# Two mixer sections reordered: input tiles and gates moved ahead of the RWKV scores and of the first chain

## The chip, the cores and the metric

The kernel runs on one core of a Trainium2 chip. The metric is the device time of one execution in microseconds (us), the median of several runs. The core has five engines with a queue of instructions each: PE (TensorE, matrix products), DVE (VectorE), ACT (ScalarE), POOL (GpSimd) and SP (SyncE, which here issues nearly all DMAs). Each works through its own queue in order, and they wait for one another through semaphores.

## The reference, cut to what matters

A hybrid encoder of two layers on 256 positions of 1024 channels, in fp32. Each layer is FFN, token mixers, FFN; the mixers are three branches on one shared input, weighted by gates:

```python
def hybrid_mixer(h, ...):                       # h: (1, 256, 1024)
    proj = h @ w_in                             # all branches' inputs and the gates
    ya = rwkv7_mixer(proj[..., :o1], ...) @ pa_w
    yb = hyena_mixer(proj[..., o1:o2], ...) @ pb_w
    yc = ssd_mixer(proj[..., o2:o3], ...) @ pc_w
    gates = jax.nn.sigmoid(proj[..., o3:]).reshape(bsz, L, N_BRANCH, D_MODEL)
    merged = gates[:, :, 0] * ya + gates[:, :, 1] * yb + gates[:, :, 2] * yc
    return merged @ w_out

def rwkv7_step(S, inp):                         # 256 steps, two directions, 8 heads of 64
    r_t, w_t, k_t, v_t, a_t, b_t = inp
    sa = jnp.einsum('dbhij,dbhj->dbhi', S, a_t)
    S = S * w_t[..., None, :] + sa[..., None] * b_t[..., None, :] + v_t[..., None] * k_t[..., None, :]
    return S, jnp.einsum('dbhij,dbhj->dbhi', S, r_t)
```

The sublayers are modulated by vectors that are themselves products of a condition with `ada_w` (`mod = cond @ ada_w[l] + ada_b[l]`). They don't depend on `x`, so the kernel computes those of later sublayers as side work.

## The kernel before, in words

`mixers(l)` writes one layer's mixers in program order; a scheduler in the framework then decides, from that order and its own estimates, in which order each engine gets its instructions. What follows is the order that came out.

The RWKV recurrence is done in chunks of 64 positions, for four heads at a time: wave 0 and wave 1. A wave has five steps. `rw_proj` computes its six input tiles; `rw_keys` the decays and keys (DVE, ACT, POOL); `rw_scores` the chunks' score matrices on PE, written to DRAM as `zin`; `rw_invert` loads `zin`, inverts triangular 32x32 blocks in 30 steps on POOL (lines 919 and 921) and stores `zout`; `rw_chain` loads `zout`, forms the chunks' inverses with 32x32 products and then goes through four chunks, one after the other. `rw_out` normalises and scales the result (a mean and a variance by matmul, DVE and ACT steps between).

Beside this stands dense work. Every column tile of `w_in` is one unit: 512 KB of weights are loaded on SP into one of four buffers named `raw` (`plain`), then PE does eight 128x256 fp32 matmuls into one of four banks (`psd`). A layer's mixers have 9 units for the RWKV inputs, 24 gates, 1 + 12 for the SSD branch (`ssd_proj`, `ssd_tiles`) and 12 for the Hyena branch (`hy_proj`). A gate is a unit, a tanh on ACT (`go`) and a store to DRAM (`gate`); `merge` loads it back as `gi`. In `merge`, the branch outputs, split into two fp32r halves (`yx`), are multiplied with the branch's output matrix (`whi`, `wlo`, loaded from `in_pab`), 8 units for each of the three branches.

`SEQ` says in which order the dense units stand behind the RWKV part in the program: ten gates, `ssd_proj` and the SSD tiles, then, after `ssd`, fourteen gates and the eight Hyena steps. Between the latter the side work (`side_work`) is spread, with a ring of three 512 KB buffers that lie where the SSD inputs were (`blk`).

The order of a mixer section on PE before the change, by the scheduler's result: inputs of wave 0, scores 0, inputs of wave 1, gates, scores 1 among gates, the rest of ten gates and the first SSD units, chain 0, chain 1 with the other dense units among their steps, output of wave 1 among the last Hyena units and the first merges, hyena, the other merges, `wout`.

Small tiles come from pools: `pt` from one that lives through the sublayer, `lt` from one that is opened after `self.arena.drop()`, in space that the arena of the RWKV part has given back.

Of the kernel before, what the change touches and what calls it, by code (L numbers as in the profile page):

```python
# [13 lines left out]
F32R = mybir.dt.float32r  # L14
# [10 lines left out]
K0 = math.exp(-0.5)  # L25


ARENA, AHEAD, BLK, START = 63 * 256, 65 * 256, 7 * 1024, 16 * 1024

KEEP, GRID = ("blk", "y0", "y1", "mg"), 256  # L30

# [8 lines left out]

NSIDE, NRING, SPOOL, NRAW, SIDEM = (4, 2, 4, 4, 1, 1), 3, (0, 0, 0, 0, 1, 0, 1, 0), 4, 3

SEQ = ("g" * 10 + "d" + "s" * 12, "g" * 14 + "h" * 8)

REL = (0, 0, 0, 0, 0, 0)

# [165 lines left out]
class Builder:  # L212
# [52 lines left out]
    def A(self, name, *shape):  # L265
        return self.arena.take(name, shape)

    def F(self, *names):
        self.arena.give(names)
# [812 lines left out]
        self.ya.append(y)  # L1082

    def out_split(self, y):
        yx = self.pt("yx", [2, 2, 256], 2, F32R)
        self.split(yx[:, 0], yx[:, 1], y)
        return [(yx[:, 0, p, :], yx[:, 1, p, :]) for p in (0, 1)]

# [55 lines left out]
    def ssd(self, l):  # L1144
        nc, A, F, bank, scol = self.nc, self.A, self.F, self.bank, self.scol

        self.yc = []
        for g in (0, 1):
            xd = A("xd", 2, 2, 256)
# [23 lines left out]
            for p in (0, 1):  # L1173
                h = 4 * g + 2 * p
# [19 lines left out]
                            self.mm(py[64 * e:64 * e + 64, p, ts], xd[:, c, d, hs], ws[:, e, n, :], n == 0, n == 2)  # L1194
                    F(f"sws{t}")
                F("svb")
            y = A("sy", 2, 256)
            for p in (0, 1):
                j = 2 * g + p
                self.stt(y[:, p, :], self.sx[:, j, :], self.dh[:, j:j + 1], py[:, p, :], MUL, ADD)  # L1200
# [7 lines left out]
            self.rsqrt(rs)  # L1208
            for p in (0, 1):
                self.stt(y[:, p, :], y[:, p, :], self.pc(l, "snw", 2 * g + p), rs, MUL, MUL)  # L1210
            self.yc += self.out_split(y)
            F("scb", "sy", "ssq", "srs", "xd")


    def hy_sin(self, x):
# [155 lines left out]
    def mixers(self, l):  # L1371
        A = self.A
        with self.phase("q") as pool:
            self.arena_open((self.pp, ARENA), (pool, AHEAD))
            blk = self.arena.sub("blk", BLK)
            st = [None, None]
            self.gd, self.mh = [None] * 3, []
            self.relief = REL[0]
            self.proj_pair(l)
            self.zz, self.ztmp = A("zz", 32, 32), A("ztmp", 240)[0:64]  # L1380
            self.rw_begin(l)
            st[0] = self.rw_proj(l, 0)
            self.rw_keys(st[0])
            self.rw_scores(st[0])
            st[1] = self.rw_proj(l, 1)
            self.relief = REL[1]
            self.rw_invert(st[0])
            self.rw_keys(st[1])
            self.rw_scores(st[1])
            self.rw_invert(st[1])  # L1390
            self.rw_chain(st[0])
            self.rw_out(st[0])
            self.F("zz", "ztmp")
            self.rw_chain(st[1])
            self.rw_out(st[1])
        self.arena.drop()
        with self.phase("w") as self.wp, self.phase("l") as self.lp:
            with self.within(blk):
                self.sx, self.sbc, self.sz = self.A("sx", 4, 256), self.A("sbc", 4, 256), self.A("sz", 4, 256)
                self.scol = self.A("scol", 3, 2, 64)  # L1400
                self.relief = REL[2]
                gates, ssd = self.gates(l), self.ssd_tiles(l)
                for c in SEQ[0]:
                    if c == "d":
                        self.ssd_proj(l)
                    else:
                        next(gates if c == "g" else ssd)
                self.relief = REL[3]
                self.ssd(l)
                self.F("sx", "sbc", "sz", "scol")  # L1410
                self.hz, self.hx = self.A("hz", 4, 256), self.A("hx", 4, 256)
                hy = self.hy_proj(l)
                names = ["cond"] + [f"ada{i}" for i in range(NRING)]
                self.cond, *self.ring = (self.A(n, 1024) for n in names)
                self.dma(self.cond, self.crow[:].to_broadcast([128, 1024]))
                self.side_begin(self.SIDE[l, 1], len(SEQ[1]))
                for c in SEQ[1]:
                    next(gates if c == "g" else hy)
                    self.side_work()
                self.side_work(True)  # L1420
                self.F(*names)
                self.ring = None
            self.mg = self.A("mg", 8, 256)
            self.relief = REL[4]
            self.merge(l, 2, self.yc, True, False)
            with self.within(blk):
                self.hyena(l)
            self.ln_begin(l, 1)
            wout = [self.ap["wout"][l, m].rearrange("p k c -> p (k c)") for m in range(8)]
            ws = [self.unit(u, ahead=NPRE) for u in wout[:NPRE]]  # L1430
            self.merge(l, 0, [x for y in self.ya for x in self.out_split(y)], False, False)
            self.merge(l, 1, [x for y in self.yb for x in self.out_split(y)], False, True)
            self.F("y0", "y1")
            self.relief = REL[5]
            for m in range(8):
                w = ws[m] if m < NPRE else self.unit(wout[m])
                pd = self.dbank()
                self.dense(pd, w, self.mh)
                self.ln_put(m, pd)
            self.early(self.ffn_units(l, 1)[:NE], NPRE)  # L1440
            self.relief = 0
            self.ln_end()
# [53 lines left out]
```

## Time and profile before

| | |
|---|---|
| three runs | 1669.35 us median, 1665.41 to 1672.22 |
| profiled execution | 1675.59 us, span 1673.7 us |
| mean granted clock of PE | 0.975 of full speed |
| busy, share of the span | PE 94%, DVE 69%, ACT 48%, POOL 16% |

The span is the time from the first to the last instruction of the profiled execution. A profile's times are from its one execution, which was 6.2 us slower than the median of the runs. In a timeline, a row is a group of instructions of one kind that follow one another on an engine, and square brackets behind it give the idle time ahead of the group and the instruction whose end released it.

### The profile page before, as it was taken

What the parts mean: (1) busy time and instruction counts of PE and PEld (TensorE: products, weight loads), DVE (VectorE), ACT (ScalarE), POOL (GpSimd) and SP (SyncE); (2) the same over time, 40 slices, a digit from 0 to 9 for tenths busy, and PEclk for the clock granted to TensorE, in tenths of its full rate; (3) what the DMA queues carried; (4) which work ended last, traced back from release to release, by engine and by line L of the source; (5) the groups of instructions that cost most, each with busy time, mean ns of one, the idle gap of its engine ahead of it and who ended that gap; (6) DMA issues with size and microseconds to landing.
All of it is one profiled execution on the core that took longest, in us unless ns stands there. A gap on an engine that the chain in (4) does not pass through costs nothing.

```text
span 1673.7 us, 31929 instructions
## 1 busy us (share of the span) xinstructions
PE 1569.5 (94%) x12118; PEld 1424.0 (85%) x12118; DVE 1150.0 (69%) x2326; ACT 801.3 (48%) x1566; POOL 267.4 (16%) x376
## 2 busy tenths in 40 slices
PE   5999999879998988899999999998999998989996
PEld 2999998768877878899999999877787787989996
DVE  6788856636446677888888887467454557876665
ACT  2655545423243535655575555452424342665554
POOL 0000013567001001100030000348620100030001
PEclk9999999989999999899999999998999999989998
DMA  9898834554548754788869986345555655666663
GB/s 376 305 324 280 282 123 155 129 127 144 169 150 288 242 170 151 282 304 295 266 220 366 315 307 199 120 106 138 156 151 158 223 188 194 189 198 221 222 177 93
DMA packets 157879, 355.74 MB, mean 213 GB/s; under 512 B 55900, under 2 KB 75805, under 8 KB 157470
## 3 DMA queue, kind: packets, MB, share of 16 engines
q1 hardware_dynamic: 157726, 353.71, 64.3%
q8 instruction: 95, 1.56, 0.4%
q14 instruction: 58, 0.48, 0.1%
HBM read 332.11 MB, written 18.91 MB: 210 GB/s over the span
## 4 chain that ended last, share of the span: by engine, by line
PE 66%; DVE 10%; POOL 9%; DMA 7%; ACT 4%; issue 3%; SPq 1%; DVEq 0%; ACTq 0%; POOLq 0%
PE psd L293 57%; PE psm L293 5%; PE pss L293 4%; POOL arena L921 3%; POOL arena L919 3%; DVE arena L282 3%; DVE arena L290 2%; DVE wlo L309 1%; SPq L296 1%; DMA arena<-in_ada 1%; ACT L279 1%; DMA gi<-gate 1%; DMA ada_raw<-in_ada 1%; ACT arena L279 1%; DMA raw<-in_pab 1%
## 5 line engine op out<-in xcount | busy, mean ns | idle before, releaser
L279 ACT ACTIVATE whi<-raw 128x512 fp32r<-128x512 f32 x608 | 370.6, 618 | 328.8 <-PE psd L293 268.2
L309 DVE TENSOR_TENSOR wlo<-raw,whi 128x512 fp32r<-128x512 f32 x608 | 405.1, 676 | 135.1 <-ACT whi L279 120.2
L293 PE MATMUL psd<-hhi,raw 128*128 128x256 f32 x1856 | 435.8, 389 | 0.7 <-DVE arena L290 0.7
L293 PEld LDWEIGHTS psd<-hhi,raw 128*128 128x128 f32 x1856 | 348.9, 192 | 63.3 <-issue 11.6
L293 PE MATMUL psd<-hhi,whi 128*128 128x256 f32 x1360 | 385.4, 285 | 9.9 <-DVE r L290 4.9
L293 PE MATMUL psd<-hhi,wlo 128*128 128x256 f32 x1360 | 384.6, 284 | 1.3 <-DVE wlo L309 1.3
L293 PE MATMUL psd<-hlo,whi 128*128 128x256 f32 x1360 | 385.5, 284 | 0.0
L293 PEld LDWEIGHTS psd<-hhi,whi 128*128 128x128 f32 x1360 | 262.0, 193 | 11.8 <-ACT sg L279 4.6
L293 PEld LDWEIGHTS psd<-hhi,wlo 128*128 128x128 f32 x1360 | 261.9, 193 | 1.6 <-DVE wlo L309 1.5
L293 PEld LDWEIGHTS psd<-hlo,whi 128*128 128x128 f32 x1360 | 262.5, 193 | 0.1
L293 PE MATMUL psd<-alo,whi 128*128 128x256 f32 x704 | 198.7, 282 | 0.0
L293 PE MATMUL psd<-ahi,wlo 128*128 128x256 f32 x704 | 197.8, 281 | 0.0
L293 PE MATMUL psd<-ahi,whi 128*128 128x256 f32 x704 | 197.4, 280 | 0.0
L581 POOL TENSOR_TENSOR r<-r,lmu 128x256 f32<-128x256 f32 x36 | 31.2, 899 | 1020.7 <-ACT lmu L279 841.3
L290 DVE SCALAR_TENSOR_TENSOR ada_raw<-ada_raw,cond 128x1024 f32<-128x1024 f32 x104 | 127.1, 1222 | 20.3 <-DMA ada_raw<-in_ada 20.1
L293 PEld LDWEIGHTS psd<-ahi,wlo 128*128 128x128 f32 x704 | 134.0, 190 | 0.3
L293 PEld LDWEIGHTS psd<-alo,whi 128*128 128x128 f32 x704 | 132.8, 189 | 0.2
L293 PEld LDWEIGHTS psd<-ahi,whi 128*128 128x128 f32 x704 | 132.2, 188 | 0.1
L293 PE MATMUL pss<-arena 128*64 128x128 f32 (+5 forms) x486 | 101.7, 385 | 26.9 <-ACT arena L279 8.6
L279 ACT ACTIVATE arena<-arena 128x512 f32<-128x512 f32 (+4 forms) x108 | 65.8, 619 | 102.5 <-DVE arena L290 35.6
L293 PEld LDWEIGHTS pss<-arena 128*64 128x64 f32 (+3 forms) x486 | 65.4, 195 | 52.1 <-issue 21.0
L293 PE MATMUL psm<-arena 32*32 32x32 f32 (+6 forms) x664 | 64.5, 263 | 28.1 <-DVE arena L290 12.6
(228 smaller groups left out, 2169.9 us busy)
## 6 DMA issues: line engine op xcount, KB each, us to landing
raw<-in_wi SPq DMA_DIRECT2D x176, 512.0 KB, 4.6
raw<-in_win SPq DMA_DIRECT2D x118, 512.0 KB, 3.8
ada_raw<-in_ada SPq DMA_DIRECT2D x104, 512.0 KB, 5.5
raw<-in_wo SPq DMA_DIRECT2D x64, 512.0 KB, 3.8
arena<-in_ada SPq DMA_DIRECT2D x32, 512.0 KB, 5.9
raw<-in_wo SPq DMA_DIRECT2D x32, 384.0 KB, 3.7
raw<-in_pab SPq DMA_DIRECT2D x24, 512.0 KB, 4.3
raw<-in_wout SPq DMA_DIRECT2D x16, 512.0 KB, 4.2
```

The source lines that it names most:

```text
L279: return self.nc.scalar.activation(out=out, in_=in_, func=func, **k)
L282: return self.nc.vector.tensor_tensor(out=out, in0=a, in1=b, op=op)
L290: return self.nc.vector.scalar_tensor_tensor(out=out, in0=a, scalar=s, in1=b, op0=op0, op1=op1, **k)
L293: return self.nc.tensor.matmul(out, lhsT, rhs, start=start, stop=stop, **k)
L296: self.nc.sync.dma_start(out, in_)
L309: return self.act(hi, src, AF.Copy), (eng or self.nc.vector).tensor_tensor(out=lo, in0=src, in1=hi.bitcast(F32), op=SUB)
L581: x = sub_(out=r[:, m, :], in0=r[:, m, :], in1=mu[:], op=SUB)
L919: g.tensor_tensor(out=tv, in0=zw[:, j + 1:32, j:j + 1].to_broadcast([64, n, j]), in1=zw[:, j:j + 1, 0:j].to_broadcast([64, n, j]), op=MUL)
L921: g.tensor_tensor(out=zw[:, j + 1:32, 0:j], in0=zw[:, j + 1:32, 0:j], in1=tv, op=ADD)
```

## The change

The six input tiles of wave 1 are written ahead of the first wave's scores instead of behind them. The gates' generator is made earlier, and `FILL` takes gates from it at two places: six ahead of the second wave's scores, eight ahead of the first chain. `SEQ` has the remaining ten, behind the SSD branch. So that this fits, the arena is five blocks larger, the SSD results (`sy0`, `sy1`) lie in it instead of being split at once, and the split (`yx`) is made when a merge needs it, from the pool `l`.

```diff
@@ -25,7 +25,7 @@
 K0 = math.exp(-0.5)
 
 
-ARENA, AHEAD, BLK, START = 63 * 256, 65 * 256, 7 * 1024, 16 * 1024
+ARENA, AHEAD, BLK, START = 68 * 256, 65 * 256, 7 * 1024, 16 * 1024
 
 KEEP, GRID = ("blk", "y0", "y1", "mg"), 256
 
@@ -40,7 +40,9 @@
 
 NSIDE, NRING, SPOOL, NRAW, SIDEM = (4, 2, 4, 4, 1, 1), 3, (0, 0, 0, 0, 1, 0, 1, 0), 4, 3
 
-SEQ = ("g" * 10 + "d" + "s" * 12, "g" * 14 + "h" * 8)
+SEQ = ("d" + "s" * 12, "g" * 10 + "h" * 8)
+
+FILL = (6, 8)
 
 REL = (0, 0, 0, 0, 0, 0)
 
@@ -1082,7 +1084,7 @@
         self.ya.append(y)
 
     def out_split(self, y):
-        yx = self.pt("yx", [2, 2, 256], 2, F32R)
+        yx = self.lt("yx", [2, 2, 256], 2, F32R)
         self.split(yx[:, 0], yx[:, 1], y)
         return [(yx[:, 0, p, :], yx[:, 1, p, :]) for p in (0, 1)]
 
@@ -1194,7 +1196,7 @@
                             self.mm(py[64 * e:64 * e + 64, p, ts], xd[:, c, d, hs], ws[:, e, n, :], n == 0, n == 2)
                     F(f"sws{t}")
                 F("svb")
-            y = A("sy", 2, 256)
+            y = self.main.take(f"sy{g}", (2, 256))
             for p in (0, 1):
                 j = 2 * g + p
                 self.stt(y[:, p, :], self.sx[:, j, :], self.dh[:, j:j + 1], py[:, p, :], MUL, ADD)
@@ -1208,8 +1210,8 @@
             self.rsqrt(rs)
             for p in (0, 1):
                 self.stt(y[:, p, :], y[:, p, :], self.pc(l, "snw", 2 * g + p), rs, MUL, MUL)
-            self.yc += self.out_split(y)
-            F("scb", "sy", "ssq", "srs", "xd")
+            self.yc.append(y)
+            F("scb", "ssq", "srs", "xd")
 
 
     def hy_sin(self, x):
@@ -1372,7 +1374,7 @@
         A = self.A
         with self.phase("q") as pool:
             self.arena_open((self.pp, ARENA), (pool, AHEAD))
-            blk = self.arena.sub("blk", BLK)
+            self.main, blk = self.arena, self.arena.sub("blk", BLK)
             st = [None, None]
             self.gd, self.mh = [None] * 3, []
             self.relief = REL[0]
@@ -1381,13 +1383,19 @@
             self.rw_begin(l)
             st[0] = self.rw_proj(l, 0)
             self.rw_keys(st[0])
+            st[1] = self.rw_proj(l, 1)
             self.rw_scores(st[0])
-            st[1] = self.rw_proj(l, 1)
             self.relief = REL[1]
             self.rw_invert(st[0])
             self.rw_keys(st[1])
+            gates = self.gates(l)
+            fill = iter(FILL)
+            for _ in range(next(fill)):
+                next(gates)
             self.rw_scores(st[1])
             self.rw_invert(st[1])
+            for _ in range(next(fill)):
+                next(gates)
             self.rw_chain(st[0])
             self.rw_out(st[0])
             self.F("zz", "ztmp")
@@ -1399,7 +1407,7 @@
                 self.sx, self.sbc, self.sz = self.A("sx", 4, 256), self.A("sbc", 4, 256), self.A("sz", 4, 256)
                 self.scol = self.A("scol", 3, 2, 64)
                 self.relief = REL[2]
-                gates, ssd = self.gates(l), self.ssd_tiles(l)
+                ssd = self.ssd_tiles(l)
                 for c in SEQ[0]:
                     if c == "d":
                         self.ssd_proj(l)
@@ -1422,14 +1430,16 @@
                 self.ring = None
             self.mg = self.A("mg", 8, 256)
             self.relief = REL[4]
-            self.merge(l, 2, self.yc, True, False)
+            both = lambda ys: [x for y in ys for x in self.out_split(y)]
+            self.merge(l, 2, both(self.yc), True, False)
+            self.F("sy0", "sy1")
             with self.within(blk):
                 self.hyena(l)
             self.ln_begin(l, 1)
             wout = [self.ap["wout"][l, m].rearrange("p k c -> p (k c)") for m in range(8)]
             ws = [self.unit(u, ahead=NPRE) for u in wout[:NPRE]]
-            self.merge(l, 0, [x for y in self.ya for x in self.out_split(y)], False, False)
-            self.merge(l, 1, [x for y in self.yb for x in self.out_split(y)], False, True)
+            self.merge(l, 0, both(self.ya), False, False)
+            self.merge(l, 1, both(self.yb), False, True)
             self.F("y0", "y1")
             self.relief = REL[5]
             for m in range(8):
```

What the scheduler makes of it. The order of SP's DMAs at the first inversion of layer 0, before (`raw_4652` and `raw_4670` are weights of SSD tiles, `zout_3557` the first inverse, `zin_3612` the second wave's input of the inversion):

```order
L296 DMA raw_4652<-in_win 128x1024
L296 DMA zout_3557<-arena_0_3094 32x1024 x2
L296 DMA raw_4670<-in_win 128x1024
L296 DMA zout_3557<-arena_0_3094 32x1024 x2
L296 DMA arena_0_3094<-zin_3612 16x32x32 x2
L296 DMA arena_1_3095<-zout_3557 32x8x32 x2
L296 DMA arena_0_3094<-zin_3612 16x32x32 x2
L296 DMA arena_1_3095<-zout_3557 32x8x32 x10
L296 DMA gate_4587<-go_4599 128x256
```

and after (`raw_3977` and `raw_3991` are the weights of gates 13 and 14, `raw_4672` those of `ssd_proj`, `zin_3697` the second wave's input, `go_3932` to `go_3974` gates 9 to 12):

```order
L298 DMA gate_3920<-go_3932 128x256
L298 DMA zout_3557<-arena_0_3094 32x1024 x4
L298 DMA gate_3920<-go_3946 128x256
L298 DMA arena_0_3094<-zin_3697 16x32x32 x4
L298 DMA gate_3920<-go_3960 128x256
L298 DMA raw_3977<-in_win 128x1024
L298 DMA raw_3991<-in_win 128x1024
L298 DMA arena_1_3095<-zout_3557 32x8x32 x4
L298 DMA arena_0_3094<-zout_3557 32x8x32
L298 DMA gate_3920<-go_3974 128x256
L298 DMA arena_0_3094<-zout_3557 32x8x32 x7
L298 DMA raw_4672<-in_wdt 128x512
```

The weights next used by PE came between the two halves of the store of `zout` and now stand behind that store and all four loads of `zin`, ahead of the loads of `zout`.

PE at the same place, before (`psd_4654` is the first SSD tile, `psm_3846` the chain's first 32x32 products):

```order
L293 MATMUL psd_4618<-hhi_3050,raw_4616 64x256
L293 MATMUL psd_4654<-hhi_3029,raw_4652 128x256
L293 MATMUL psd_4654<-hhi_3032,raw_4652 128x256
L293 MATMUL psd_4654<-hhi_3035,raw_4652 128x256
L293 MATMUL psd_4654<-hhi_3038,raw_4652 128x256
L293 MATMUL psm_3846<-arena_1_3095 32x32 x2
L293 MATMUL psd_4654<-hhi_3041,raw_4652 128x256
L293 MATMUL psd_4654<-hhi_3044,raw_4652 128x256
L293 MATMUL psm_3846<-arena_1_3095 32x32 x30
L293 MATMUL psd_4654<-hhi_3047,raw_4652 128x256
```

and after (`psd_3965`, `psd_3979`, `psd_3993` are gates 12, 13, 14; `psm_4005` transposes for the chain; `psm_4044` its first 32x32 products; `psd_4674` is `ssd_proj`):

```order
L295 MATMUL psd_3965<-hhi_3050,raw_3963 128x256
L295 MATMUL psm_4005<-cst,arena_0_3094 64x64 x16
L295 MATMUL psd_3979<-hhi_3029,raw_3977 128x256
L295 MATMUL psd_3979<-hhi_3032,raw_3977 128x256
...
L295 MATMUL psd_3993<-hhi_3047,raw_3991 128x256
L295 MATMUL psd_3993<-hhi_3050,raw_3991 128x256
L295 MATMUL psm_4044<-arena_1_3095 32x32 x32
L295 MATMUL psd_4674<-hhi_3029,raw_4672 64x256
```

Two whole gates now stand between the transposes and the first 32x32 products. By the whole order, 112 dense matmuls of gates and later units stand ahead of these products, where 92 stood; 278 dense matmuls instead of 280 come between them and the end of the second chain (276 instead of 274 in layer 1), and 2 instead of 20 behind it (4 instead of 26 in layer 1). When the second scores end, nine more dense matmuls have been placed than before.

PE at the end of the second chain in layer 0, before (`psd_5432` is the last Hyena unit, `psm_4447` the mean in the output of wave 1, `psd_5461` the first merge, `yx_4939` half of the split SSD output):

```order
L293 MATMUL psd_5432<-hhi_3032,raw_5430 128x256
L293 MATMUL psd_5432<-hhi_3035,raw_5430 128x256
L293 MATMUL psm_4447<-arena_0_3094,cst 128x512
L293 MATMUL psd_5432<-hhi_3038,raw_5430 128x256
L293 MATMUL psd_5432<-hhi_3041,raw_5430 128x256
L293 MATMUL psd_5432<-hhi_3044,raw_5430 128x256
L293 MATMUL psd_5432<-hhi_3047,raw_5430 128x256
L293 MATMUL psd_5432<-hhi_3050,raw_5430 128x256
L293 MATMUL psd_5461<-yx_4939,whi_5453 128x256 x2
L293 MATMUL psd_5461<-yx_4939,wlo_5454 128x256
L293 MATMUL psd_5461<-yx_4939,whi_5453 128x256 x2
```

and after (`psm_4645` to `psm_4661` are the output of wave 1, the `pss` tiles are hyena's, `yx_5443` is the split SSD output):

```order
L295 MATMUL psd_5426<-hhi_3047,raw_5424 128x256
L295 MATMUL psd_5426<-hhi_3050,raw_5424 128x256
L1302 MATMUL pss_5617<-cst,arena_0_3094 128x128 x4
L1302 MATMUL pss_5623<-cst,arena_0_3094 128x128 x4
L295 MATMUL psm_4645<-arena_0_3094,cst 128x512
L295 MATMUL psm_4649<-arena_1_3095,cst 128x512
L295 MATMUL psm_4657<-arena_0_3094,cst 128x512
L295 MATMUL psm_4661<-arena_0_3094 128x256 x2
L295 MATMUL pss_5631<-arena_0_3094 128x512 x2
L295 MATMUL pss_5634<-arena_0_3094 128x512 x2
L295 MATMUL psd_5461<-yx_5443,whi_5453 128x256
L295 MATMUL psd_5477<-yx_5443,whi_5457 128x256
```

The output's matmuls stood singly among dense ones and merges; now they stand in a row, the merges come behind all of them, and the first hyena products stand on both sides. On SP, eight of the sixteen side loads of layer 0 now stand behind the last weights from `in_win`, among the merges' weights and ahead of hyena's `in_fwd`; before, none did.

## Rows read from the trace of the kernel before

**Rows 1.** The page's head: span; busy time, share, instructions of engines.

```profile
span 1673.7 us, 31929 instructions
...
PE 1569.5 (94%) x12118; PEld 1424.0 (85%) x12118; DVE 1150.0 (69%) x2326; ACT 801.3 (48%) x1566; POOL 267.4 (16%) x376
```

**Rows 2.** The chain that ended last, its shares by engine.

```profile
PE 66%; DVE 10%; POOL 9%; DMA 7%; ACT 4%; issue 3%; SPq 1%; DVEq 0%; ACTq 0%; POOLq 0%
```

**Rows 3.** Windows, busy time: chains and tail, layer 0, then layer 1.

```profile
core 0: us, PE busy (x) PEld busy (x) DVE busy (x) ACT busy (x) POOL busy (x), PEclk, DMA share, GB/s
...
391.80:556.00 164.20, 156.49 (x1347) 127.65 (x1345) 93.01 (x230) 56.56 (x113) 27.38 (x39) 0.99 0.59 194
556.00:623.40 67.40, 62.02 (x388) 53.45 (x386) 48.66 (x101) 29.45 (x53) 0.00 (x0) 0.95 0.56 187
...
1203.50:1360.40 156.90, 153.88 (x1355) 125.48 (x1353) 83.31 (x215) 54.22 (x109) 23.14 (x37) 1.00 0.56 176
1360.40:1429.90 69.50, 63.35 (x400) 54.73 (x398) 50.39 (x105) 30.65 (x55) 0.00 (x0) 0.98 0.58 189
```

**Rows 4.** PE's timeline, layer 0, at the scores: start, duration, group, idle.

```profile
276.78 15.38 PE L293 MATMUL psd<-hhi,raw 128*128 128x256 f32 x70
295.24 0.71 PE L293 MATMUL psm<-arena 64*128 64x128 f32 x4 [3.09 <-DVE arena L290]
...
337.51 1.22 PE L293 MATMUL psm<-arena 64*128 64x128 f32 x4 [5.12 <-DVE arena L290]
```

**Rows 5.** PE's timeline, layer 0, at the chain's first products.

```profile
365.76 2.30 PE L293 MATMUL psd<-hhi,raw 128*64 128x256 f32 x9
373.85 0.64 PE L293 MATMUL psm<-arena 32*32 32x32 f32 x4 [5.79 <-DMA arena<-zin]
374.42 2.08 PE L293 MATMUL psd<-hhi,raw 128*128 128x256 f32 x4
```

**Rows 6.** PE's timeline, layer 1, second scores to the chain's first products.

```profile
1147.45 0.71 PE L293 MATMUL psm<-arena 64*128 64x128 f32 x4 [1.29 <-DVE arena L290]
...
1158.13 0.46 PE L889 MATMUL psm<-cst,arena 64*128 64x64 f32 x4 [3.70 <-DVE arena L282]
...
1176.80 7.84 PE L293 MATMUL psd<-hhi,raw 128*128 128x256 f32 x34
1185.67 0.21 PE L293 MATMUL psm<-arena 32*32 32x32 f32 x2 [1.02 <-issue]
```

**Rows 7.** SP's DMA issues, layer 0, at the first inversion's end.

```profile
366.08 0.79 SPq L296 DMA_DIRECT2D zout<-arena  x2
...
368.06 0.77 SPq L296 DMA_DIRECT2D zout<-arena  x2
...
371.16 0.97 SPq L296 DMA_DIRECT2D arena<-zin  x2
```

**Rows 8.** The page's DMA issues: size, median us from issue to landing.

```profile
raw<-in_win SPq DMA_DIRECT2D x118, 512.0 KB, 3.8
```

**Rows 9.** SP's DMA issues, layer 1, the last load of zin.

```profile
1183.17 0.97 SPq L296 DMA_DIRECT2D arena<-zin  x2
```

**Rows 10.** Windows, ten microseconds around the wait of 5.79 us.

```profile
370.00:380.00 10.00, 6.10 (x79) 4.72 (x80) 0.18 (x1) 4.67 (x6) 2.23 (x9) 0.66 0.55 107
```

**Rows 11.** DVE's timeline, layer 0, first and last step of the second wave's output.

```profile
559.24 0.69 DVE L282 TENSOR_TENSOR arena<-arena 128x512 f32<-128x512 f32 x1
...
576.05 0.68 DVE L282 TENSOR_TENSOR arena<-arena,psm 128x512 f32<-128x512 f32 x1
```

**Rows 12.** PE's timeline, layer 0: the output's mean, and hyena's inverse.

```profile
562.55 1.02 PE L293 MATMUL psm<-arena,cst 128*128 128x512 f32 x2
...
604.30 8.28 PE L293 MATMUL pss<-arena 128*128 128x256 f32 x24 [3.92 <-DVE gi L290]
```

**Rows 13.** SP's issues, layer 0: first and last load of the side work.

```profile
502.49 0.32 SPq L296 DMA_DIRECT2D arena<-crow  x1
...
543.82 0.38 SPq L296 DMA_DIRECT2D arena<-in_ada  x1
```

## The prediction

> **What bounds the kernel now.** I read the page's head first: TensorE (PE) is busy for 1569.5 of 1673.7 us [rows 1], and the chain that ended last lies on it for 66%, on DVE, POOL and DMA for 26% together [rows 2]. So PE is the bound, and what an order can win is PE's idle time; the total of its matmuls is the same after the change. Then I cut each mixer section at three points, where one first-wave chain begins, where the second chain ends and where the last merge ends, and asked for the busy time of each stretch [rows 3]. In the chain stretch PE idles for 164.20 - 156.49 = 7.7 us in layer 0 and 156.90 - 153.88 = 3.0 us in layer 1, in the tail (chain's end to the last merge) for 5.4 and 6.2 us. The rest of the idle time lies ahead of the chain; PE's timeline there shows three waits in layer 0: 3.09 us ahead of the first wave's scores, 5.12 us ahead of the second's [rows 4], 5.79 us ahead of the chain's first products, which are released by DMA [rows 5]. In layer 1 they are smaller, and one of them is DVE's, inside the second scores [rows 6].
>
> A dense matmul (one of the eight 128x256 fp32 products of an input tile or a gate, two records each) takes 15.38 us for 35 of them [rows 4], 0.44 us each. All terms below use that price.
>
> **The change part by part.**
>
> Second-wave input tiles ahead of the first scores: seven dense matmuls (3.1 us) come to stand in the wait of 3.09 us. They came after it before, so PE has them behind it. But what ends next is DVE's: the second scores begin when DVE has their operands, 5.12 us after PE has run dry [rows 4]. DVE has the same work in the same order there, so I let that point stand still. What counts is how much dense work is done by then. By the order nine more dense matmuls (4.0 us) are done when scores of wave 1 end, and the waits to hold them are there: 5.12 us in layer 0, 1.29 + 3.70 in layer 1 [rows 4, 6]. Gain: 4.0 us in each layer, bounds 0 and 4.0 (nothing, if DVE is delayed as well).
>
> Gates ahead of the chain: by the order 92 dense matmuls stand before the chain's first 32x32 products now, 112 afterwards. The 20 cost 8.8 us, against the 4.0 just won. Their weights decide. On SP's queue those of gates 13 and 14 now stand behind the store of the first inverse (zout) and the loads of the second (zin). The store is issued at 366.08 and 368.06, when the inversion on POOL is through, and the last zin pair at 371.16 with 0.97 us [rows 7]. One gate store and one issue behind it (0.4 us each, half of the 0.79 for two) put the weights' issue near 372.5; with 3.8 us to landing [rows 8] they are there at 376.3. PE ended its dense work at 368.06 with 92 matmuls done [rows 5]; with 96 (twelve gates) and nine of them covered it comes to gate 13 at 368.06 + 1.8 - 4.0 = 365.9. It then waits 10.4 us, where it waited 5.79, and everything behind, the chain's products too, waits with it. The first products follow 16 matmuls (7.0 us) later, at 383.3 instead of 373.85: **+9.5 us in layer 0**. In layer 1 the last zin pair is issued at 1183.17 [rows 9], so the weights land near 1188.7. PE ended at 1176.80 + 7.84 = 1184.6 [rows 6], so it comes to gate 13 at 1182.4 and waits 6.3 us. The first products stand at 1195.7 instead of 1185.67: **+10.0 us**.
>
> The clock: after the wait of 5.79 us two dense matmuls take 2.08 us [rows 5], 1.04 each instead of 0.44, and the ten microseconds around show a mean granted clock of 0.66 [rows 10], part of the stretch at 1.2 instead of 2.4 GHz. So a cold start costs about 1.2 us by that row. Layer 0 pays it before and after; layer 1, which had only 1.02 us of wait, pays it new: +1.2, bounds 0 and 2.4.
> The Trainium skill, in "TensorE: Matmul & The Clock Gate", section "HAM oscillation — how this bites in real kernels", says that matmuls which must wait for a DMA find the clock throttled when they start again, and pay for the transition at every such wait; its example has 1.67 us at half rate per wait, a loss of some 0.8 us as an estimate. The row of the 5.79 us wait agrees in kind; by the page's figure the sum would be 0.4 us lower.
>
> The chain stretch: between the chain's first products and its end PE has 278 dense matmuls in layer 0 where it had 280 (-0.9 us), 276 where it had 274 in layer 1 (+0.9). Its waits I leave as they are; bounds: all 7.7 and 3.0 us of idle time go, or as much comes on top.
>
> The tail: 18 dense matmuls less in layer 0 (2 instead of 20, -7.9 us), 22 less in layer 1 (4 instead of 26, -9.7). But these and the merges of the SSD branch covered the chain of DVE, ACT and PE steps that is the second wave's output. That chain ended at 576.05 + 0.68 = 576.7 [rows 11], 20.7 us after the stretch's start at 556.0. Its first matmul only began at 562.55 [rows 12], behind dense ones, although its operand was ready at 559.24 + 0.69 = 559.9; without them it ends some 2.6 us earlier, at 18.1. The split of the SSD output (yx), which the merges read, is now written behind that chain, as its pool lies where the chain's tiles lay, and takes another half microsecond or so (a DVE step of that width is 0.68). So the first merge can't run on before some 18.7 us. In the order PE has ahead of it 2 dense matmuls (0.9), eight transposes, four hyena products of 128x512 (1.02 each by the nearest row [rows 12], 4.1) and the output's own (about 4): together, with an estimate of 1.7 for the transposes, 10.7 us. That leaves 8 us of waiting. The side work (modulation of later sublayers) adds to it in layer 0: now it runs from 502.49 to past 543.82, fifteen loads in 41 us [rows 13], and its end leaves 12 us to the chain's end. In the new order eight of its loads stand behind the last input weights, among the merges' weights and ahead of hyena's, and its DVE products stand between the output's steps. I add 3 us: 11 us of waiting instead of 5.4, bounds 0 and 20. In layer 1, with half as many side loads and with more of hyena ahead of the merges (about 15 us in all), I take 3.5 instead of 6.2. The 3.92 us before hyena's inverse [rows 12] go with the new order in both cases. Tail: -7.9 + 5.6 = -2.3 in layer 0, -9.7 - 2.7 = -12.4 in layer 1.
>
> Sum: layer 0 +9.5 - 0.9 - 2.3 = +6.3; layer 1 +10.0 + 1.2 + 0.9 - 12.4 = -0.3. Together **+6.0 us**. The profiled execution (1675.59 us, 1.9 us of them around its span) would come to 1681.6. It lies 6.2 us above the median of the runs shown, 1669.35, so runs should have a median of **1675 us**. A measurement here tells about 0.5% (8.3 us) from no change.
>
> **The rivals.**
> - *The weights are there in time* (faster). If gate 13's weights land before PE comes to it, the 16 matmuls run in what were waits: the chain in layer 0 starts at 373.85 as now (365.9 + 7.0 is before that), 9.5 us better, and in layer 1 at 1189.4, 7.5 us better with its cold start. Sum 6.0 - 17.0 = -11.0: 1658 us. For it: before, gate weights were issued between the zout pairs, and the inversion's end could come earlier. Against: the order of one queue, and POOL's inversion is untouched. It decides at a landing by 366 and 1182.4. Chance 0.20.
> - *The tail is covered* (no change or faster). If yx is ready when PE comes to the merges, 11 and 3.5 us go: 1661 us. Half of it gives 1668. For it: the output chain waits for PE now at two places. Against: the yx pool's address. Chance 0.15; a third of that is beyond the bound.
> - *Side work ends the tail* (slower by more than the bound). If the side products, and hyena's loads behind them on SP, are not done before about 18 us after the chain's end, every further microsecond is one of PE's. Eight loads at 41/15 = 2.7 us, from the last input weights on, which are issued some 10 us before the chain's end, end at 12 us; with DVE taken by the output's steps this can become 28: +10, 1685 us. For it: nothing in the new order lets these loads go earlier. Against: in layer 1 there is half as much of it, and loads may start before the last input weights do. Chance 0.25.
> - The forecast, 1668 to 1683, has the remaining 0.40.
>
> **How the numbers follow.** Of the forecast's 0.40 I put 0.28 within the bound (1668 to 1677.7) and 0.12 above it; the covered tail's 0.15 is 0.10 within and 0.05 below. So faster has 0.20 + 0.05 = 0.25, the same 0.28 + 0.10 = 0.38, slower 0.12 + 0.25 = 0.37. The range takes the forecast, the covered tail, and most of both outer rivals, with the bounds of the tail's wait: 1657 to 1689. The likeliest case alone: 1668 to 1683.
>
> **What would show it.** Right: near 366 in layer 0 PE stops before a dense matmul of a gate, released by the DMA of its weights at about 376, and near 1182 again for about 6 us; the waits at 292 and 332 are gone or near 1 us; the first 32x32 products stand near 383 and 1196 (plus any shift of what comes before); after the second chain's end PE waits around the output steps, for about 11 us in layer 0, and the merges run on without the 3.92 us wait. Wrong: no PE wait for weights there, or yx ready at once, makes it faster; a wait in the tail that is ended by a side load or a hyena load makes it slower; so would second scores that start later because DVE was held up by the earlier input tiles.

## The result and the profile after

Seven runs of the changed kernel have a median of 1678.49 us (1671.43 to 1679.25), seven of the kernel before 1669.35 us (1664.44 to 1672.22). The ratio is 1.0052, 95% interval 1.003 to 1.0074: slower by 0.5%, some 9 us, where the prediction had 6 us. The profiled execution of the changed kernel took 1678.84 us, close to its median; that of before lay 6 us above its own. So the two spans differ by 3.4 us only (1677.1 and 1673.7); in a second profiled execution of each kernel, below, they differ by 5.8.

The page's head and the shares of the chain that ended last, of the changed kernel, against [rows 1, 2]:

```profile
span 1677.1 us, 31931 instructions
...
PE 1568.3 (94%) x12118; PEld 1421.6 (85%) x12118; DVE 1147.9 (68%) x2326; ACT 802.6 (48%) x1566; POOL 264.7 (16%) x376
...
PE 73%; DVE 8%; DMA 7%; POOL 6%; ACT 3%; issue 2%; SPq 1%; ACTq 0%; DVEq 0%; POOLq 0%
```

PE has the same work, so the time is in its waits. To see where, I cut each layer's mixers at the section's first matmul, the chain's first 32x32 products, the end of the second chain and the end of the last merge; the last two of the three stretches are called the chain stretch and the tail. First the kernel before, layer 0 and then layer 1 (us, then busy time and count of each engine, granted clock, DMA):

```profile
259.60:373.80 114.20, 99.33 (x588) 81.48 (x588) 64.34 (x91) 48.85 (x99) 62.41 (x83) 0.94 0.51 138
373.80:556.00 182.20, 173.24 (x1561) 141.11 (x1561) 102.22 (x250) 65.35 (x127) 40.01 (x65) 0.98 0.59 192
556.00:623.50 67.50, 62.10 (x388) 53.45 (x386) 48.66 (x101) 29.50 (x54) 0.00 (x0) 0.95 0.56 187
1073.00:1185.60 112.60, 103.18 (x589) 83.87 (x588) 62.93 (x91) 48.89 (x99) 61.24 (x83) 0.92 0.52 139
1185.60:1360.40 174.80, 169.05 (x1549) 137.76 (x1549) 92.50 (x235) 62.96 (x122) 35.67 (x63) 0.99 0.56 173
```

(the sixth, layer 1's tail, is the last of [rows 3]). The same stretches of the changed kernel:

```profile
258.40:385.90 127.50, 111.38 (x629) 91.80 (x628) 63.61 (x88) 51.82 (x102) 69.47 (x103) 0.91 0.52 141
385.90:556.10 170.20, 168.16 (x1558) 137.39 (x1557) 98.64 (x244) 61.61 (x121) 26.72 (x44) 1.00 0.56 177
556.10:627.20 71.10, 57.86 (x350) 46.37 (x350) 52.07 (x109) 31.31 (x56) 4.70 (x2) 0.88 0.63 213
1075.40:1201.70 126.30, 110.13 (x629) 90.82 (x627) 60.86 (x88) 51.65 (x102) 68.92 (x103) 0.92 0.52 143
1201.70:1369.50 167.80, 167.08 (x1554) 136.57 (x1553) 95.20 (x241) 61.01 (x120) 26.59 (x44) 1.00 0.54 170
1369.50:1433.10 63.60, 55.30 (x356) 46.99 (x354) 47.51 (x98) 29.68 (x53) 0.00 (x0) 0.97 0.61 191
```

Beside the prediction's terms (the last column is from a second profiled execution of each kernel, below):

| stretch | predicted | measured | second time |
|---|---|---|---|
| layer 0, to the first 32x32 products | +9.5 | +13.3 | +13.8 |
| layer 0, chains | -0.9 | -12.0 | -8.6 |
| layer 0, tail | -2.3 | +3.6 | -2.3 |
| layer 1, to the first 32x32 products | +11.2 | +13.7 | +12.6 |
| layer 1, chains | +0.9 | -7.0 | -6.8 |
| layer 1, tail | -12.4 | -5.9 | -4.5 |
| sum | +6.0 | +5.7 | +4.2 |

The two pairs of traces so show 4 to 6 us in the mixers, of the 5 to 12 that the runs tell; where the rest lies isn't shown.

The first term stands in PE's timeline where it was forecast. Layer 0 and layer 1, against [rows 5, 6]:

```profile
365.66 1.15 PE L295 MATMUL psm<-cst,arena 64*64 64x64 f32 x32
376.83 9.16 PE L295 MATMUL psd<-hhi,raw 128*128 128x256 f32 x32 [10.03 <-DMA raw<-in_win]
385.92 0.78 PE L295 MATMUL psm<-arena 32*32 32x32 f32 x64
...
1192.60 9.17 PE L295 MATMUL psd<-hhi,raw 128*128 128x256 f32 x32 [10.02 <-DMA raw<-in_win]
1201.70 0.78 PE L295 MATMUL psm<-arena 32*32 32x32 f32 x64
```

PE stops for 10.03 us at gate 13, released by its weights at 376.83 (forecast 376.3), does 16 cold matmuls in 9.16 us (cold: at a lower clock, a mean granted 0.78 of full speed here) and comes to the chain at 385.92 (forecast 383.3). SP shows why, against [rows 7]:

```profile
366.07 2.71 SPq L298 DMA_DIRECT2D zout<-arena  x4
368.88 0.37 SPq L298 DMA_DIRECT2D gate<-go  x1
369.35 2.04 SPq L298 DMA_DIRECT2D arena<-zin  x4
371.43 0.48 SPq L298 DMA_DIRECT2D gate<-go  x1
371.96 0.93 SPq L298 DMA_DIRECT2D raw<-in_win  x2
```

The two weights are issued at 371.96, behind the store that waited for POOL's inversion until 366.07 and behind the loads of zin.

The tail of layer 0, on PE, against [rows 12]:

```profile
561.85 2.05 PE L295 MATMUL psm<-arena,cst 128*128 128x512 f32 x2 [3.85 <-DVE arena L284]
565.34 3.61 PE L295 MATMUL psm<-arena,cst 128*128 128x512 f32 x4 [1.45 <-ACT arena L281]
...
576.28 6.66 PE L295 MATMUL pss<-arena 128*128 128x512 f32 x8 [6.47 <-DMA arena<-in_fwd]
```

The three waits make 11.8 us; the forecast was 11. But the longest is not for yx: it is hyena's load of `in_fwd`. DVE's timeline there:

```profile
571.72 1.22 DVE L292 SCALAR_TENSOR_TENSOR arena<-arena 128x1024 f32<-128x1024 f32 x1
572.87 0.08 DVE L292 DVE_READ_ACCUMULATOR arena<-arena 128x1 f32 x1
```

and SP's:

```profile
572.97 0.62 SPq L298 DMA_DIRECT2D arena<-in_fwd  x1
```

The load goes out as soon as the last side product has ended (571.72 + 1.22 = 572.94), as it is written where the side work's buffers lay.

### The profile page after: what moved, and what is told of

Its sections match the earlier page's. It is cut to its first block, busy times and chain, and to the rows that moved or that the text cites. A ratio compares the mean times of both kernels' runs of the same rounds, so it can differ in the third digit from the quotient of the medians.

```text
span 1677.1 us, 31931 instructions
## 1 busy us (share of the span) xinstructions
PE 1568.3 (94%) x12118; PEld 1421.6 (85%) x12118; DVE 1147.9 (68%) x2326; ACT 802.6 (48%) x1566; POOL 264.7 (16%) x376
## 4 chain that ended last, share of the span: by engine, by line
PE 73%; DVE 8%; DMA 7%; POOL 6%; ACT 3%; issue 2%; SPq 1%; ACTq 0%; DVEq 0%; POOLq 0%
PE psd L295 62%; PE psm L295 6%; PE pss L295 5%; POOL arena L923 2%; POOL arena L921 2%; DVE arena L292 2%; DVE arena L284 2%; DVE wlo L311 2%; SPq L298 1%; DMA gi<-gate 1%; ACT L281 1%; DMA raw<-in_win 1%; DMA ada_raw<-in_ada 1%; DMA arena<-arena 1%; ACT arena L281 1%
## 5 line engine op out<-in xcount | busy, mean ns | idle before, releaser
L295 PEld LDWEIGHTS pss<-arena 128*64 128x64 f32 (+3 forms) x486 | 60.4, 180 | 54.6 <-issue 24.3
L295 PE MATMUL psm<-arena 128*64 128x64 f32 (+5 forms) x1072 | 71.9, 239 | 7.4 <-ACT arena L281 3.5
```

What stands on the lines that cost most here:

```text
L295: return self.nc.tensor.matmul(out, lhsT, rhs, start=start, stop=stop, **k)
```

## The experiments

The theory: the change costs time because the weights of gates 13 and 14 stand on SP behind DMAs that wait for POOL, and because layer 0's side work now ends in the tail. The main rival: the chain can't use an earlier start, and what is won ahead of it comes back as waits inside it. All ratios are against the kernel before, run beside; the changed kernel's is 1.0052, and where a run is set against the changed kernel, its ratio is divided by this one.

**e1, e2, e3: the inversion's DMAs on ACT.** In `rw_invert` (e1):

```diff
-                self.dma(dst[32 * d + 16 * h:32 * d + 16 * h + 16], src)
+                self.nc.scalar.dma_start(dst[32 * d + 16 * h:32 * d + 16 * h + 16], src)
...
-            self.dma(zout[d, 32 * d:32 * d + 32], zw[32 * d:32 * d + 32])
+            self.nc.scalar.dma_start(zout[d, 32 * d:32 * d + 32], zw[32 * d:32 * d + 32])
...
-            self.dma(zout[1 - d, 32 * d:32 * d + 32], zo[32 * d:32 * d + 32])
+            self.nc.scalar.dma_start(zout[1 - d, 32 * d:32 * d + 32], zo[32 * d:32 * d + 32])
```

e2 does the same, beside this, to the loads of `zout` in `rw_chain`; e3 is e2's edit made to the kernel before.

> The changed kernel, with the inversion's loads of zin and stores of zout issued from ACT instead of SP; PE's order stays the same but for two of the chain's 16 transposes. Theory: the weights of gates 13 and 14 were late only because they stood behind these DMAs on SP. Then the waits of 10.0 us ahead of gate 13 go in both layers, and the chain's first 32x32 products come at about 375 instead of 385.9 in layer 0 and about 1191 instead of 1201.7 in layer 1. The twelve loads of zout still stand on SP ahead of ssd_proj's weights, so a part of it, up to 6 us a layer, may come back ahead of ssd_proj; time 1662 to 1672 us. Rival: the chain can't begin earlier anyway, or what it wins comes back as waits inside the chain (9.0 and 5.8 us before the change); then the time stays within 0.3% of the changed kernel's 1678.

> As the run before, and the chain's twelve loads of zout on ACT as well, so that SP has nothing of the inversion. Theory: also no wait ahead of ssd_proj; first 32x32 products at 375 and 1191, chain stretches as short as in the changed kernel (170 and 168 us), time 1658 to 1666 us. Rival as before; a further one is that ACT, which issues them one by one (about 0.5 us each), holds up the tanh of the gates and so PE's banks: PE would then wait for ACT at dense matmuls and the time would be above 1670.

> Control: the same DMAs on ACT in the kernel before. Its PE waits there (5.8 and 1.0 us) were on the inversion itself and not on weights, so both theories expect little: within 0.3% of 1669. If it gains as much as the changed kernel does, the gain has nothing to do with the gates' weights.

e1: 1674.12 us, ratio 1.0034 (1.0019 to 1.0048). e2: 1667.70, 0.9994 (0.9978 to 1.0011). e3: 1672.47, 1.0015 (1.0 to 1.003). The 10 us waits are gone, but e1 and e2 are slower than expected (1662 to 1672 and 1658 to 1666). The longest of PE's waits in e1's layer 0 up to 392 us (us in total, times, longest):

```profile
PE psm L295 <- DVE arena L292: 11.5, 1, 11.5
PE psd L295 <- DMA raw<-in_wdt: 4.5, 1, 4.5
PE psd L295 <- DMA raw<-in_win: 1.1, 1, 1.1
```

4.5 us for ssd_proj's weights was expected, and is gone in e2. The 11.5 us is new, and stands in e2 as well (11.7): PE waits for the second wave's operands, and the second scores begin 83.5 us after the section's start instead of 77.0. ACT stands idle for 3.57 us around the issue of two of the first wave's loads of `zin` (314.41), and DVE's part of the operands begins 60.8 us after the section's start instead of 59.1. That is 1.6 of the 6.5 us. The larger part is DVE's own: from there the same steps take 21.6 us instead of 16.8 (319.38 to 340.99, against 317.53 to 334.36). The first inversion on POOL begins 2.7 us earlier there (59.7 instead of 62.4 us after the section's start) and runs beside more of them; whether that slows them no run tests. So the edit brought a wait of its own; the control e3, whose second scores are later too (80.4 instead of 77.9), is no faster than the kernel before.

**e6: without the first wave's loads of `zin`.** Stores of `zout`, the second wave's `zin` and the first chain's `zout` loads on ACT (the last stood behind the gates' weights on SP, ahead of those of `ssd_proj`):

```diff
-                self.dma(dst[32 * d + 16 * h:32 * d + 16 * h + 16], src)
+                (self.nc.scalar if w else self.nc.sync).dma_start(dst[32 * d + 16 * h:32 * d + 16 * h + 16], src)
...
-                self.dma(zp[part, 2 * h:2 * h + 2].rearrange(
+                (nc.sync if w else nc.scalar).dma_start(zp[part, 2 * h:2 * h + 2].rearrange(
```

and so for the other lines that load `zout`; its stores as in e1.

> The changed kernel with only those DMAs on ACT that stood ahead of the gates' weights: the stores of zout, the second wave's loads of zin, and the first chain's loads of zout; the first wave's loads of zin stay on SP, since on ACT they held the second scores up by 6.5 us. Theory: no wait of 10 us ahead of gate 13, second scores where the changed kernel has them (77.0 us after the section's start); first 32x32 products 114 to 118 us after the section's start instead of 127.5; 7 to 12 us less than that kernel's 1678 in each layer's first part, and since the chains then run beside side work and inversions as before, 1660 to 1668 us in all. Rival: it comes back as waits in the chain stretch; then 1672 or more.

1664.85 us, ratio 0.9983 (0.997 to 0.9997), 0.7% below the changed kernel. PE in layer 0:

```profile
364.36 3.69 PE L295 MATMUL psd<-hhi,raw 128*128 128x256 f32 x16 [1.13 <-DMA raw<-in_win]
368.91 3.72 PE L295 MATMUL psd<-hhi,raw 128*128 128x256 f32 x16 [0.86 <-ACT go L281]
...
376.86 0.31 PE L295 MATMUL psm<-arena 32*32 32x32 f32 x2 [2.97 <-DMA arena<-zout]
```

Gates 13 and 14 run where PE stood still, and the second scores are back at 76.7 us after the section's start. The chain stretches, from 116.0 and 114.3 us after the section's start:

```profile
373.60:551.30 177.70, 170.77 (x1561) 138.73 (x1557) 98.04 (x244) 66.06 (x128) 34.85 (x63) 0.98 0.57 177
1182.00:1356.50 174.50, 170.57 (x1555) 138.82 (x1553) 94.09 (x241) 65.91 (x128) 35.27 (x63) 0.98 0.55 173
```

Here the rival has a part. The chains start 11.5 and 12.0 us sooner, but their stretches are 7.5 and 6.7 us longer than the changed kernel's with the same units in them: 5 us more idle time in layer 0 (6.9 instead of 2.0), 3.2 in layer 1, the rest a lower granted clock. 4 and 5.3 us a layer are kept; the tails are 1 us shorter. PE's waits in these stretches, all of layer 0 and the longest of layer 1:

```profile
PE psm L295 <- DMA arena<-zout: 4.2, 2, 3.0
PE psm L295 <- DVE arena L1008: 2.1, 2, 1.4
PE psm L295 <- DVE rw_rhs L1003: 0.3, 1, 0.3
PE pss L1122 <- DVE arena L288: 0.2, 1, 0.2
...
PE psm L295 <- DMA arena<-zout: 2.5, 1, 2.5
```

So what came back is for the most part one wait for `zout` behind the first four products, and the low clock that follows it (a mean of 0.65 from 373.6 to 380 us, 0.80 from there to 386); the waits of the chain's later steps are little longer than in the changed kernel (2.7 us against 2.0, and 1.4 against 0.7).

**e4, e5: half of layer 0's side work moved to the FFN ahead,** in the changed kernel and in the one before:

```diff
-NSIDE, NRING, SPOOL, NRAW, SIDEM = (4, 2, 4, 4, 1, 1), 3, (0, 0, 0, 0, 1, 0, 1, 0), 4, 3
+NSIDE, NRING, SPOOL, NRAW, SIDEM = (5, 1, 4, 4, 1, 1), 3, (0, 0, 0, 0, 1, 0, 1, 0), 4, 3
```

> The changed kernel with half of layer 0's side work (eight of sixteen loads) moved from its mixers to the FFN ahead of them. Theory: the tail of layer 0 (71.1 us) was ended by the last side product, behind which hyena's load of in_fwd waits (6.47 us); it becomes like layer 1's (63.6 us): about 7 us less in this stretch, and 3 to 8 us less in all, by what the first FFN pays. Rival: the tail is set by the output's own chain and the split behind it; then the wait for in_fwd only turns into one for yx and the tail loses less than 2 us.

> Control for the run with less side work: the kernel before with the same move of eight side loads from layer 0's mixers to the FFN ahead. In the kernel before the side work ended 12 us ahead of the chain's end, so by my theory it gains at most the 4.5 us which one chain step waited for DVE behind side products, less what the FFN pays: ratio to before 0.996 to 1.001. If it gains as much as the changed kernel did (12.6 us, 0.75%), that gain says nothing about the tail of the changed kernel.

e4: 1665.93 us, 0.998 (0.9967 to 0.9993), 0.7% below the changed kernel. e5: 1667.72, 0.9998 (0.9982 to 1.0014): nothing. So the move helps the changed kernel and not the one before; 12 us are more than the 3 to 8 expected. In e4 the wait for `in_fwd` is 1.5 us instead of 6.47, layer 0's tail 67.4 us instead of 71.1. That and 2.4 us in its chain stretch are half of the 12 us that the runs show (give or take 4); in which stretch the rest lies, one trace doesn't settle.

**e7: e6 and e4 together.**

> The run before and half of layer 0's side work moved to the FFN: both costs taken away. Theory: the two add up: 10 to 13 us less than the run without the side move has over the changed kernel, so 1650 to 1658 us. Rival: the side move's gain was due to the chain's later start; then it gains no more than 3 us here.

1656.46 us, ratio 0.9925 (0.9906 to 0.9943): the fastest of all, 0.75% faster than the kernel before and 1.3% faster than the changed one. Layer 0's tail in it, and the weights of gates 13 and 14 on SP:

```profile
549.00:611.20 62.20, 54.77 (x354) 46.05 (x354) 47.34 (x99) 28.63 (x51) 0.00 (x0) 0.97 0.59 190
```

```profile
359.41 0.93 SPq L298 DMA_DIRECT2D raw<-in_win  x2
```

They go out at 359.41, 12.5 us sooner than in the changed kernel, and the tail is 8.9 us shorter than there. Against e6, 7.7 of the 8.9 us that the six stretches are shorter lie in this tail (62.2 instead of 69.9 us), which ties the gain of the side move to it better than e4's one trace. The two costs were separate ones.

**e8, e9, e10: the parts of the change.** e8 has `FILL = (6, 6)` and twelve gates in `SEQ[1]`; e9 `FILL = (0, 0)` and `SEQ` of before; e10 the changed kernel with

```diff
-            st[1] = self.rw_proj(l, 1)
             self.rw_scores(st[0])
+            st[1] = self.rw_proj(l, 1)
```

> The changed kernel with six gates instead of eight ahead of the first chain (twelve behind the SSD branch): gates 13 and 14 don't stand ahead of the chain's 32x32 products. Theory: the 10 us wait for their weights goes; the products wait about 8 us for the loads of zout instead and begin near 375 in layer 0; but 88 of the chain's matmuls follow in a row without dense work between them, and ssd_proj's weights come behind twelve loads of zout, so some 6 to 10 us of waiting come back there: 1670 to 1678 us. Rival (the late start of the chain is what costs): 8 us less in each layer, below 1664.

> The changed kernel without its fill: no gate is written ahead of the second scores or of the first chain, the order behind the chains is that of the kernel before (ten gates, SSD, fourteen gates and Hyena); input tiles early and the split from the other pool remain. PE's order then has 96 dense matmuls ahead of the chain's 32x32 products (112 in the changed kernel, 92 before), and no gate whose weights stand behind the inversion's DMAs. Theory: first products about 116 us after the section's start instead of 127.5, the tail between that of before and of the changed kernel; 1660 to 1668 us, so the fill itself costs about 10 us. Rival: the early input tiles and the pool cost as much; then 1672 or more.

> The changed kernel with the second wave's input tiles back behind the first scores; fill and pool stay. Gates 12, 13 and 14 then stand between the chain's transposes and its 32x32 products, 112 dense matmuls ahead of them as in the changed kernel. Theory: the wait ahead of the first scores (3.1 us) comes back, but the second scores are set by DVE; so what it had behind it, seven matmuls, is done later in a wait: 0 to 3 us a layer, 1677 to 1685 us. Rival: early tiles only cost; then 2 us a layer less than 1678.

e8: 1664.81 us, 0.9968 (0.9954 to 0.9983). e9: 1665.55, 0.9962 (0.9946 to 0.9979). e10: 1679.57, 1.0057 (1.0041 to 1.0073). Without gates 13 and 14 ahead of the chain, the change is 0.3 to 0.4% faster than the kernel before; with them, 0.5% slower. The early tiles alone don't show in e10 against the changed kernel; they can't, as the chain waits for gate 13's weights in both, and what is won ahead of that wait only lengthens it (11.50 us in e10's layer 0, 10.03 there). What makes e9 faster than the kernel before, the tiles, the split's pool or the larger arena, no run takes apart. e8 is faster than I expected. Its PE in layer 0:

```profile
376.95 1.47 PE L295 MATMUL psm<-arena 32*32 32x32 f32 x64 [10.45 <-DMA arena<-zout]
```

The wait is as long as in the changed kernel, 10.45 us, and now for `zout` itself; but the chain begins at its end and not 16 cold matmuls later, and of the 6 to 10 us that I saw coming back behind it only 3.6 did (0.56, 1.22, 0.96 and 0.86 us ahead of the chain's next steps and ssd_proj). e9's chain stretches, from 112.6 and 111.3 us after the section's start, with the dense units in the order of the kernel before:

```profile
369.60:549.20 179.60, 173.24 (x1559) 141.67 (x1559) 96.34 (x247) 62.37 (x122) 41.05 (x65) 0.97 0.61 191
1180.90:1355.20 174.30, 169.69 (x1551) 139.32 (x1551) 88.65 (x236) 60.02 (x117) 36.63 (x63) 0.98 0.57 175
```

PE is idle in them for 6.4 and 4.6 us.

**e11, e12: both kernels profiled once more.**

> The kernel before, profiled once more. Its first profiled execution was 6 us above the median of its runs, and its first-chain-to-second-chain stretch in layer 0 took 182.2 us, where two relatives with the same units there took 174.5 and 172.7. If that was this execution's own (a wait of 4.5 us for DVE among side products), the stretch is now 173 to 177 us and the span 1664 to 1670; if it belongs to the kernel, it is 181 to 183 again.

> The changed kernel, profiled once more: the waits of 10 us for gate 13's weights in both layers and the wait for in_fwd in layer 0's tail (6 to 7 us) should stand again, first products at 126 to 128 us after the section's start, chain stretches 167 to 171 us, span 1672 to 1678. If the wait for in_fwd were this execution's own, the tail would be below 67 us.

Before again: span 1670.7 us, layer 0's chain stretch 178.2 us; it came down by 4 us and not to the 173 to 177 expected. The wait of 4.5 us for DVE in its second chain is 1.2 us this time, so most of it was that execution's. After again: span 1676.5 us, chains 169.6 and 167.0 us, waits of 9.7 us for gate 13's weights in layer 0 and 6.2 us for `in_fwd`: as the first time. In layer 1 the wait at gate 13 is 9.6 us, and the profile puts its end down to ACT's copy of `zin` (L916); in e6's layer 0 gate 13 begins at 364.36 and that copy at 376.53, so the gate doesn't depend on it. The chain stretches of layer 0, before and after:

```profile
374.40:552.60 178.20, 173.31 (x1561) 141.03 (x1561) 98.15 (x250) 65.39 (x127) 40.07 (x65) 0.98 0.61 193
388.50:558.10 169.60, 168.10 (x1558) 137.40 (x1557) 97.93 (x244) 61.62 (x121) 24.98 (x42) 1.00 0.57 177
```

## Why the prediction was right, and where its steps were not

The direction, the size (6 us forecast, 9 with an interval of 5 to 12 measured) and the likeliest case held. Its main mechanism is shown: e6, e8 and e9 each take the two gates' weights out of the way by another means and each come out 0.7 to 0.9% below the changed kernel. The sum came out near, though, because errors of its terms cancelled: +3.8, -11.1 and +5.9 us in layer 0, +2.5, -7.9 and +6.5 in layer 1. That is luck.

- *Wait for the weights.* 10.4 us forecast, 10.03 measured in layer 0. In layer 1, 6.3 forecast, 10.02 measured: the store of `zout` went out at 1181.85 instead of 1178.13, 1.3 us later even against the section's start, and PE came to gate 13 some 2 us sooner than forecast. From the weights' issue to PE's start 4.87 us passed in both layers, where I had 3.8 (and, in layer 1 alone, one issue of 0.4 us too many).
- *The cold start* was mis-sized: 16 matmuls took 9.16 us instead of 7.0, so 2.1 us (2.8 and 2.4 in the second execution) where I put 1.2 from a row that held only two matmuls. In layer 0 it also changed its place: before, it stood behind the first products, in the chain stretch (a mean granted clock of 0.66 in the first 6.2 us of it), and now ahead of them. The Trainium skill's figure ("TensorE: Matmul & The Clock Gate", section "HAM oscillation — how this bites in real kernels"), from which I estimated 0.8 us, was lower still; the measurement decides. The rule itself, that a wait for a DMA is paid for again by slow matmuls behind it, agrees with these rows.
- *The chain stretch* is the step that failed. I left its waits as they were, though the dense units among its steps had changed. PE's idle time there fell from 9.0 to 2.0 us and from 5.8 to 0.7 (in the second executions from 4.9 to 1.5 and from 4.7 to 0.3), and the clock rose to 1.00, in layer 0 in good part because the cold start left the stretch. My bounds of 7.7 and 3.0 us of idle time were read from windows that begin 18 us behind the first products; they end at -8.6 and -2.1 us, and layer 1's -7.0 and -6.8 lie far beyond. That the late start took these waits away isn't shown. e6 starts early with the same units and has, without its wait for `zout`, 2.7 and 1.4 us of idle time; e9 starts early with the units in the order of the kernel before and has 6.4 and 4.6. So these runs speak for the order of the units as the cause; none changes that order alone.
- *The tail.* In layer 0 the size of the wait was nearly right (11 forecast, 11.8 in three waits, 13.2 of idle time in all); its largest part was hyena's load behind the last side product, which I had as the mechanism of the slower rival, at 10 us on top; e4 and e7 show it. I had put nothing for the clock there: the matmuls between and behind the waits ran cold (2.05 us for two records that took 1.02 in [rows 12]), at a mean of 0.88 in the stretch instead of 0.95. In layer 1 the tail had 8.3 us of idle time instead of 3.5, in six waits of 2.5 us and less; with its 22 dense matmuls less it gained 5.9 us (4.5 the second time), less than half of the 12.4 forecast.
- *Early tiles.* The 4.0 us a layer were right on average only: PE came to gate 13 108.4 us after the section's start in layer 0 (106.3 forecast) and 107.2 in layer 1 (109.4 forecast), so 1.9 and 6.2 us were won. In the sum they count for nothing, as the weights' landing sets the chain's start; e10 finds no gain for the same reason.

The rival "weights in time" had 1658 us; e6, which makes it true, took 1665: right in sign, and 7 us too good. I had the products where they stood before; in e6 most of them waited for `zout` until 378.35, and the chain stretch gives back part of what was won.

## What to carry to other kernels

Work put into a wait only pays if its operands are there by then: look at the queue that loads them, and at what that queue's next DMA waits for, not at the order of the engine that computes. What is put ahead of a serial chain and doesn't fit the wait delays the chain's start by its whole length; how much of that is lost is read at the chain's end (12 us sooner at the start were 4 and 5 us there in e6). Work that is moved away from the end may uncover something that had been hidden there (here side work and a load into its buffers), so read what ends last in the stretch it left.

## What the runs showed of the hardware

An idle spell of 10 us cost 2.1 us more in each layer: 9.16 and 9.17 us for 16 matmuls that take 7.0, at a mean granted clock of 0.78 and 0.77 (9.85 and 9.40 us in the second execution); behind a wait of 1.07 us, in e1, the same 16 took 7.14. A DMA issued from ACT holds ACT up while it waits: in e1 ACT stood idle for 3.57 us around two loads of `zin`. The second scores came 6.5 us later by this edit, 1.6 of them because DVE began later and 4.8 because the same DVE steps took longer, which isn't explained. Executions of one kernel differ in single waits by several microseconds (4.5 and 1.2 us at one chain step), so a stretch's difference of 3 or 4 us between two traces is not yet a finding.
